# A blocked triangular inverse with two token tiles to a PSUM bank, its transfers on GpSimd's queue, and recurrence decays in tiles of their own

## The chip, the cores and the metric

One core of a Trainium2 chip runs the whole program: four layers of a sequence model on 512 tokens of width 1024. The metric is the device time of one execution in microseconds; the kernel before takes 1904.87 us, the median of three runs (1903.52 to 1909.27).

## What is computed

The first two layers (differential attention and a long convolution) are not touched. Each of the last two has three branches on the same normed input: a gated delta rule (GDN), a causal latent attention (MLA) and a gated linear recurrence (RG-LRU). The parts of the reference that matter:

```python
# gated delta rule, chunks of 64 tokens, 4 heads
a_mat = where(strict, einsum('bnhid,bnhjd->bnhij', kbeta, kc) * decay, 0) + eye(C)
rhs = concatenate([vc * bc, kbeta * exp(gc)[..., None]], axis=-1)
sol = lax.linalg.triangular_solve(a_mat, rhs, lower=True, unit_diagonal=True)
u, w = sol[..., :DV], sol[..., DV:]
...
# rg_lru
r = sigmoid(einsum('bsnc,ncd->bsnd', xb, w_r) + b_r)
i = sigmoid(einsum('bsnc,ncd->bsnd', xb, w_i) + b_i)
log_a = -RG_C * r * softplus(-a_param)
a = exp(log_a)
b = sqrt(-expm1(2.0 * log_a)) * (i * x)
h = associative_scan(a1 * a2, a2 * b1 + b2) over the tokens
```

The kernel solves the triangular system by making the inverse of `a_mat` and multiplying by it. It works on tiles of 128 tokens, so each inverse is 128x128.

## The kernel before, in words

Projections are fp32 split into two parts and multiplied in three passes (`mm3`, L258 to L260); a weight chunk is loaded by SyncE, cast by ScalarE (L266) and its remainder made by VectorE or, for every third chunk, by GpSimd (L267).

In each of the last two layers `layer2` calls `gdn_front`, `lru_open`, `gdn`, `lru`, `mla_v` and `mla` in that order. The framework puts the instructions of each engine in one fixed order before the program runs: by its own estimate of time, an engine takes the ready instruction that was traced earliest. Work that was traced later (projections of `lru`, `mla_v`, `mla`) so fills the places in which earlier work waits. On the chip every engine then follows that order and waits where it must.

The steps around the change, for one layer:

- `solve32` (L1383 to L1401) inverts the 32x32 diagonal blocks on VectorE with 62 small operations (L1398, L1400) and writes them to DRAM (`dm`) by a DMA on ScalarE's queue (L1401).
- `spread` (L1409 to L1427) reads the blocks back by six more DMAs on ScalarE's queue: two into `xd` (L1420), four into `xc` (L1422, named go in the profile). Each moves 64 KB as runs of 32 floats. VectorE then transposes them into `xtc` and the diagonal of `XT` (L1424, L1426).
- `gdn` makes four output gates, then runs `gdn_inv` for the four token tiles (i = 0 to 3) as four generators in turn (`pipeline`, L1474): step 1 of all tiles, then step 2 of all tiles, and so on.
- `gdn_inv` has five steps. Step 1: matmuls L1439 into a bank `lg`, copied by ScalarE (L1441). Step 2: L1445 and L1447 into a bank that the profile calls ft or tr, copied by ScalarE (L1451, L1453), with two small GpSimd operations (L1449, L1450). Step 3: L1457, L1458. Step 4: L1462, L1463. Step 5: L1467, L1471 and their copies. `lg` has two buffers; tr and ft have one each, taken in turn. The matmuls of steps 1, 3 and 4 have 64 columns, those of step 2 have 32, those of step 5 have 128. The first step may not be issued before the last projection of `lru_open` (`self.after(lead)`).
- `lru` takes its four channel chunks in two pairs. Of a chunk: two gate matmuls (L1230, L1233) with a Tanh each (L1232, L1234), Exp for the decay (L1237), Tanh and Sqrt (L1238, L1241), the products (L1235, L1243, L1244), the scan (L1245), a projection for the output gate (L1247, silu at L701 and L702) and the last product (L1250). Tag `l` has three buffers, tag `g2` five, `lw` and bank `av` one each. The decay `dc` has its tile from `g2` and shares it with the second Tanh. The Sqrt of both chunks of a pair are traced together. In `mla` the first user of an `l` tile is L1124.

The lines that the texts below speak of beside these: L1518 (GpSimd, state of the recurrence), L486 (DMAs that GpSimd issues in the first two layers).

Of the kernel before, what the change touches and what calls it, by code (L numbers as in the profile page):

```python
# [12 lines left out]
AF = mybir.ActivationFunctionType  # L13
# [155 lines left out]
class Kern:  # L169
# [1044 lines left out]
    def lru(self, l, h, opened):  # L1214
        nc, A = self.nc, self.A
        bh, sp2, ny, us, conv, _ = opened
        o = self.U()
        for pair in ((0, 1), (2, 3)):
            ts = {}
            for c in pair:  # L1220
                w = self.T("lw", (P, 2, P))
                nc.gpsimd.memset(w, 0.0)
                for q in range(2):
                    r = slice(64 * q, 64 * q + 64)
                    nc.sync.dma_start(w[r, :, r], A[f"lw{l}"][q][:, c])
                if c == 2:
                    conv(3)
                u = us[c]
                pr, pi = self.ps("av"), self.ps("av")
                nc.tensor.matmul(pr, w[:, 0], u, start=True, stop=True)  # L1230
                t, dc = self.T("l"), self.T("g2")
                nc.scalar.activation(t, pr, AF.Tanh, scale=0.5, bias=bh[:, c:c + 1])  # L1232
                nc.tensor.matmul(pi, w[:, 1], u, start=True, stop=True)  # L1233
                nc.scalar.activation(dc, pi, AF.Tanh, scale=0.5, bias=bh[:, 4 + c:5 + c])  # L1234
                nc.vector.scalar_tensor_tensor(u, dc, 1.0, u, op0=ADD, op1=MUL)  # L1235

                nc.scalar.activation(dc, t, AF.Exp, scale=ny[:, c:c + 1], bias=ny[:, c:c + 1])  # L1237
                nc.scalar.activation(t, t, AF.Tanh, scale=sp2[:, c:c + 1], bias=sp2[:, c:c + 1])  # L1238
                ts[c] = t, dc, u
            for t, _, _ in ts.values():  # L1240
                nc.scalar.activation(t, t, AF.Sqrt, scale=0.25)  # L1241
            for c, (t, dc, u) in ts.items():
                nc.vector.scalar_tensor_tensor(t, dc, 1.0, t, op0=ADD, op1=MUL)  # L1243
                nc.gpsimd.tensor_tensor(u, u, t, op=MUL)  # L1244
                nc.vector.tensor_tensor_scan(t, dc, u, 0.0, op0=MUL, op1=ADD)  # L1245
                ps = self.ps("acc")
                self.projT(self.wchunk(A[f"xin{l}"][28 + c], 8, P), h, ps)  # L1247
                gz = self.T("l")
                self.silu2(gz, ps)
                nc.gpsimd.tensor_tensor(o[:, c], t, gz, op=MUL)  # L1250
# [132 lines left out]
    def solve32(self, l, at):  # L1383

        nc = self.nc
        for k in range(4):
            nc.scalar.dma_start(self.blk(self.da[l], k), self.diag(at, k))
        w = self.U()[0:64].rearrange("p (n a) (b i) -> p n (a b) i", n=2, i=32)
        a, m = w[:, 0], w[:, 1]
        flat = lambda t: t.rearrange("p i c -> p (i c)")  # L1390
        nc.scalar.dma_start(flat(a), self.da[l])
        nc.gpsimd.memset(flat(m), 0.0)
        nc.gpsimd.memset(flat(m)[:, 0::33], 1.0)
        tmp = self.T("st", (P, 256))[0:64]
# [14 lines left out]
    def spread(self, l):  # L1409


        nc = self.nc
        xtc, xc = (self.T("go", (P, 16, 32)) for _ in range(2))
        xd = self.T("xd", (P, 16, 64))
        XT = self.T("XT", (P, 4, 4, P))
        nc.gpsimd.memset(XT, 0.0)
        nc.gpsimd.memset(xd, 0.0)
        rs = lambda k: slice(32 * k, 32 * k + 32)
        for k in (0, 2):
            nc.scalar.dma_start(xd[rs(k), :, 16 * k:16 * k + 32], self.blk(self.dm[l], k))  # L1420
        for k in range(4):
            nc.scalar.dma_start(xc[rs(k)], self.blk(self.dm[l], k))  # L1422

        nc.vector.transpose(xtc, xc)  # L1424
        for k in range(4):
            nc.vector.transpose(self.diag(XT, k), xc[rs(k)])  # L1426
        return xd, xc, xtc, XT  # L1427

    def gdn_inv(self, i, at, t1, X, kb, v2, lead):

        nc = self.nc
        mm = nc.tensor.matmul
        ts = slice(i * P, (i + 1) * P)
        xd, xc, xtc, XT = X
        xi = xd[:, 4 * i:4 * i + 4]
        p1 = self.ps("lg", (P, 4, 64))
        with self.after(lead):
            for c in range(4):
                mm(p1[:, c], at[:, i, c], xd[:, 4 * i + c], start=True, stop=True)  # L1439
        for b in (0, 64):  # L1440
            nc.scalar.activation(t1[b + 32:b + 64, i, :, b:b + 32], p1[b + 32:b + 64, :, b // 2:b // 2 + 32], AF.Copy)  # L1441
        yield
        p2 = self.ps("tr", (P, 2, 4, 32))
        for c in range(4):
            mm(p2[:, 0, c], XT[:, i, c], t1[:, i, c, 0:32], start=True, stop=True)  # L1445
        for c in range(4):
            mm(p2[:, 1, c], t1[:, i, c], xtc[:, 4 * i + c], start=True, stop=True)  # L1447

        nc.gpsimd.memset(xi[64:96, :, 32:64], 0.0)  # L1449
        nc.gpsimd.tensor_copy(xi[32:64, :, 32:64], xc[32:64, 4 * i:4 * i + 4])  # L1450
        nc.scalar.activation(xi[32:64, :, 0:32], p2[32:64, 0], AF.Copy, scale=-1.0)  # L1451
        for b in (0, 64):
            nc.scalar.activation(XT[b:b + 32, i, :, b + 32:b + 64], p2[b:b + 32, 1], AF.Copy, scale=-1.0)  # L1453
        yield
        p3 = self.ps("lg", (P, 4, 64))
        for c in range(4):
            mm(p3[:, c], at[:, i, c], xd[:, 4 * i + c], start=True, stop=True)  # L1457
        nc.scalar.activation(t1[64:128, i, :, 0:64], p3[64:128], AF.Copy)  # L1458
        yield
        p4 = self.ps("tr", (P, 4, 64))  # L1460
        for c in range(4):
            mm(p4[:, c], t1[:, i, c], XT[:, i, c, 64:128], start=True, stop=True)  # L1462
        nc.scalar.activation(XT[0:64, i, :, 64:128], p4[0:64], AF.Copy, scale=-1.0)  # L1463
        yield
        pw = self.ps("lg", (P, 4, P))
        for c in range(4):
            mm(pw[:, c], kb[:, i, c], XT[:, i, c], start=True, stop=True)  # L1467
        nc.scalar.activation(kb[:, i], pw, AF.Copy)
        pu = self.ps("tr", (P, 4, P))
        for c in range(4):  # L1470
            mm(pu[:, c], XT[:, i, c], v2[:, c, ts], start=True, stop=True)  # L1471
        nc.scalar.activation(v2[:, :, ts], pu, AF.Copy)

    def pipeline(self, live):  # L1474

        while live:
            live = [g for g in live if next(g, self) is not self]

    def gdn(self, l, h, lead, q2, k2, v2, at, an, kb, egs, ssq, t1, X):
        nc, A = self.nc, self.A  # L1480
        mm = nc.tensor.matmul
        gz = self.U()
        for c in range(4):
            ps = self.ps("acc")
# [14 lines left out]
        for i in range(4):  # L1499
            ts = slice(i * P, (i + 1) * P)  # L1500
            eg = egs[:, i]
            po = self.ps("tr", (P, 4, P))
            for q in range(2):
                hs = slice(2 * q, 2 * q + 2)
                s1 = st[q]
                ps = self.ps("lg", (P, 2, P))
# [25 lines left out]
            r = self.sm(4, "hr")  # L1532
# [129 lines left out]
```

## Time and profile before

| | us |
|---|---|
| median of the runs | 1904.87 (1903.52 to 1909.27) |
| the profiled execution, its own time | 1900.04 |
| its span, first to last instruction | 1898.3 |
| TensorE busy | 1859.4 (98%) |
| VectorE, ScalarE, GpSimd busy | 1246.5, 901.0, 654.3 |
| mean granted TensorE clock | 0.989 |

What lies around the span is 1.7 us. In the profile PE is TensorE's matmul, PEld its weight load, DVE VectorE, ACT ScalarE, POOL GpSimd, SP SyncE; a q behind a name is the engine's sequencer, which issues DMAs and waits. PEclk is the granted clock as a share of full speed: 1.00 is 2.4 GHz, 0.50 is 1.2 GHz.

### The profile page before, as it was taken

The page shows a single profiled execution, that of the slowest core. Times are in us where ns is not written, and L with a number is a line of the kernel's source. Part 1 is how long each engine was busy: PE and PEld are TensorE (multiplying, and loading weights), DVE is VectorE, ACT ScalarE, POOL GpSimd, SP SyncE. Part 2 cuts the span into 40 slices and gives each one's busy share as a digit, 9 for nine tenths or more (in the row PEclk, how much of TensorE's full clock was granted, in tenths as well). Part 3 has the DMA queues.
Part 4 walks back from the last instruction along what each step waited for, and adds up shares of the span by engine and source line. Part 5 has one row for each costly group of instructions (what it writes and reads, how often), then busy time and mean ns, then how long its engine had stood idle before and what let it go on. Part 6 is the DMA issues. An engine that isn't in the chain of part 4 may idle for free.

```text
span 1898.3 us, 26049 instructions
## 1 busy us (share of the span) xinstructions
PE 1859.4 (98%) x9604; PEld 1567.9 (83%) x9604; DVE 1246.5 (66%) x2238; ACT 901.0 (47%) x1761; POOL 654.3 (34%) x552
## 2 busy tenths in 40 slices
PE   8999999999999999999999999999999999999998
PEld 5878888887788788888888788888888887888886
DVE  6888688665788759765567935657235794465723
ACT  4766432324576632223455346656325534765631
POOL 2355343542245534443147323111114642311110
PEclk9999999999999999999999979999999998999999
DMA  5333433224333352333332221213343232022242
GB/s 176 108 111 110 150 113 109 101 89 169 112 99 104 106 169 97 104 100 130 117 103 71 89 61 36 73 59 113 102 136 103 76 89 71 26 76 63 74 133 89
DMA packets 81609, 190.84 MB, mean 101 GB/s; under 512 B 21858, under 2 KB 31843, under 8 KB 81481
## 3 DMA queue, kind: packets, MB, share of 16 engines
q1 hardware_dynamic: 69448, 184.71, 29.8%
q10 hardware_dynamic: 10880, 2.36, 0.7%
q0 software_dynamic: 1152, 2.10, 0.4%
q8 instruction: 76, 1.25, 0.3%
q14 instruction: 53, 0.43, 0.1%
HBM read 171.29 MB, written 17.84 MB: 100 GB/s over the span
## 4 chain that ended last, share of the span: by engine, by line
PE 74%; DVE 14%; issue 4%; ACT 3%; POOL 2%; DMA 2%; ACTq 0%; SPq 0%; DVEq 0%; POOLq 0%
PE acc L260 12%; PE acc L258 12%; PE acc L259 12%; PE fl L260 5%; PE fl L258 5%; PE fl L259 5%; PE av L1181 2%; DVE wl L267 2%; PE av L259 1%; PE av L258 1%; PE av L260 1%; PE lg L260 1%; PE lg L259 1%; PE lg L258 1%; DVE g L1005 1%
## 5 line engine op out<-in xcount | busy, mean ns | idle before, releaser
L266 ACT ACTIVATE wh<-wr 128x1024 fp32r<-128x1024 f32 (+3 forms) x268 | 256.4, 957 | 453.6 <-PE acc L259 165.4
L258 PE MATMUL acc<-u,wh 128*128 128x512 f32 x996 | 394.5, 396 | 0.2
L259 PE MATMUL acc<-u,wh 128*128 128x512 f32 x996 | 393.1, 395 | 0.0
L260 PE MATMUL acc<-u,wl 128*128 128x512 f32 x996 | 393.0, 395 | 0.0
L267 POOL TENSOR_TENSOR wl<-wr,wh 128x1024 fp32r<-128x1024 f32 (+3 forms) x86 | 185.4, 2155 | 498.9 <-ACT wh L266 456.8
L267 DVE TENSOR_TENSOR wl<-wr,wh 128x1024 fp32r<-128x1024 f32 (+3 forms) x182 | 216.0, 1187 | 169.4 <-ACT wh L266 162.1
L258 PEld LDWEIGHTS acc<-u,wh 128*128 128x128 f32 x996 | 187.2, 188 | 41.4 <-issue 2.3
L260 PEld LDWEIGHTS acc<-u,wl 128*128 128x128 f32 x996 | 187.2, 188 | 40.0 <-issue 3.1
L259 PEld LDWEIGHTS acc<-u,wh 128*128 128x128 f32 x996 | 187.3, 188 | 37.1 <-issue 1.4
L258 PE MATMUL fl<-u,wh 128*128 128x512 f32 x316 | 127.7, 404 | 0.0
L260 PE MATMUL fl<-u,wl 128*128 128x512 f32 x316 | 127.1, 402 | 0.0
L259 PE MATMUL fl<-u,wh 128*128 128x512 f32 x316 | 126.9, 402 | 0.0
L260 PE MATMUL acc<-wh,u 128*128 128x512 f32 (+1 forms) x212 | 79.7, 376 | 0.3
L259 PE MATMUL acc<-wl,u 128*128 128x512 f32 (+1 forms) x212 | 79.0, 373 | 0.0
L258 PE MATMUL acc<-wh,u 128*128 128x512 f32 (+1 forms) x212 | 77.7, 374 | 0.6 <-ACT u L266 0.5
L260 PEld LDWEIGHTS fl<-u,wl 128*128 128x128 f32 x316 | 60.4, 191 | 14.0 <-issue 2.0
L258 PEld LDWEIGHTS fl<-u,wh 128*128 128x128 f32 x316 | 60.3, 191 | 14.0 <-issue 2.4
L259 PEld LDWEIGHTS fl<-u,wh 128*128 128x128 f32 x316 | 60.2, 191 | 13.3 <-issue 2.0
L677 ACT ACTIVATE p<-p,mx 128x512 f32<-128x512 f32 x64 | 45.8, 717 | 36.9 <-DVE mx L675 36.6
L790 POOL TENSOR_TENSOR w<-w,ab 128x256 f32<-128x256 f32 x32 | 39.4, 1232 | 68.5 <-DVE w L789 63.3
L321 ACT ACTIVATE sq<-x 128x512 f32<-128x512 f32 x40 | 25.3, 632 | 68.2 <-DVE x L1615 38.1
L1168 ACT ACTIVATE p<-p,amx 128x128 f32<-128x128 f32 (+1 forms) x64 | 35.9, 562 | 30.6 <-DVE amx L1167 29.9
(633 smaller groups left out, 4440.0 us busy)
## 6 DMA issues: line engine op xcount, KB each, us to landing
wr<-in_win SPq DMA_DIRECT2D x88, 512.0 KB, 3.5
wr<-in_xin SPq DMA_DIRECT2D x64, 512.0 KB, 3.5
wr<-in_xout SPq DMA_DIRECT2D x32, 512.0 KB, 3.5
hd<-f SPq DMA_DIRECT2D x32, 256.0 KB, 3.7
hs<-hd SPq DMA_DIRECT2D x32, 256.0 KB, 2.7
wr<-in_wout SPq DMA_DIRECT2D x16, 512.0 KB, 3.4
xd<-x SPq DMA_DIRECT2D x12, 512.0 KB, 3.2
x<-xd SPq DMA_DIRECT2D x12, 512.0 KB, 3.4
```

The lines of the kernel that those rows point to most:

```text
L258: mm(ps, l[0], r[0], start=first, stop=False)
L259: mm(ps, l[0], r[1], start=False, stop=False)
L260: return mm(ps, l[1], r[0], start=False, stop=last)
L266: nc.scalar.activation(hi, src, AF.Copy)
L267: (nc.gpsimd if pool else nc.vector).tensor_tensor(lo, src, hi.bitcast(F32), op=SUB)
L321: self.nc.scalar.activation(self.T("sq"), self.xt(i)[:, h * S:(h + 1) * S], AF.Square, scale=1.0 / math.sqrt(D), accum_out=self.ms2[i][:, ...
L677: nc.scalar.activation(pp[c], pp[c], AF.Exp, bias=mx[:, c:c + 1], accum_out=s0[:, i:i + 1] if c == 0 else s)
L790: nc.gpsimd.tensor_tensor(a[:, 0], a[:, 0], b[:, 1], op=ADD)
L1005: nc.vector.scalar_tensor_tensor(y[:, d:], ps[:, :S - d], w(n), y[:, d:], op0=MUL, op1=ADD)
L1168: nc.scalar.activation(p[:, :n], p[:, :n], AF.Exp, bias=mx, scale=scale, accum_out=s)
L1181: mm(po[:, ts], v[hd // 4][:, k, (hd % 4) * P:(hd % 4 + 1) * P], w[:, k], start=k == 0, stop=k == i)
```

## The change

`gdn_inv` is one function with plain loops: each step runs over the four tiles. For steps 1 to 4 the banks are taken ahead, two for a step, and tiles 0 and 1 share the first, 2 and 3 the second. The seven DMAs of `solve32` and `spread` behind the VectorE part are issued by GpSimd. In `lru` the pairs are gone; a chunk's second Tanh has its tile from `g2` (`ti`) and the decay has one from `l` (`dc`); the Sqrt follows in the chunk. `pipeline` is removed. The numbers of matmuls and copies stay.

```diff
     def lru(self, l, h, opened):
-        for pair in ((0, 1), (2, 3)):
-            ts = {}
-            for c in pair:
+        for c in range(4):
 ...
-                t, dc = self.T("l"), self.T("g2")
+            t, ti, dc = self.T("l"), self.T("g2"), self.T("l")
 ...
-                nc.scalar.activation(dc, pi, AF.Tanh, scale=0.5, bias=bh[:, 4 + c:5 + c])
-                nc.vector.scalar_tensor_tensor(u, dc, 1.0, u, op0=ADD, op1=MUL)
+            nc.scalar.activation(ti, pi, AF.Tanh, scale=0.5, bias=bh[:, 4 + c:5 + c])
+            nc.vector.scalar_tensor_tensor(u, ti, 1.0, u, op0=ADD, op1=MUL)
 ...
-            for t, _, _ in ts.values():
-                nc.scalar.activation(t, t, AF.Sqrt, scale=0.25)
-            for c, (t, dc, u) in ts.items():
-                nc.vector.scalar_tensor_tensor(t, dc, 1.0, t, op0=ADD, op1=MUL)
+            nc.scalar.activation(t, t, AF.Sqrt, scale=0.25)
+            nc.vector.scalar_tensor_tensor(t, dc, 1.0, t, op0=ADD, op1=MUL)
 ...
     def solve32(self, l, at):
 ...
-        nc.scalar.dma_start(self.dm[l], flat(m))
+        nc.gpsimd.dma_start(self.dm[l], flat(m))
 ...
     def spread(self, l):
 ...
         for k in (0, 2):
-            nc.scalar.dma_start(xd[rs(k), :, 16 * k:16 * k + 32], self.blk(self.dm[l], k))
+            nc.gpsimd.dma_start(xd[rs(k), :, 16 * k:16 * k + 32], self.blk(self.dm[l], k))
         for k in range(4):
-            nc.scalar.dma_start(xc[rs(k)], self.blk(self.dm[l], k))
+            nc.gpsimd.dma_start(xc[rs(k)], self.blk(self.dm[l], k))
 ...
-    def gdn_inv(self, i, at, t1, X, kb, v2, lead):
+    def gdn_inv(self, lead, at, t1, X, kb, v2):
 ...
-        p1 = self.ps("lg", (P, 4, 64))
-        with self.after(lead):
-            for c in range(4):
-                mm(p1[:, c], at[:, i, c], xd[:, 4 * i + c], start=True, stop=True)
-        for b in (0, 64):
-            nc.scalar.activation(t1[b + 32:b + 64, i, :, b:b + 32], p1[b + 32:b + 64, :, b // 2:b // 2 + 32], AF.Copy)
-        yield
+        def banks(tag, shape):
+            ps = [self.ps(tag, (P, 2) + shape) for _ in range(2)]
+            return [ps[i // 2][:, i % 2] for i in range(4)]
+
+        p1 = banks("lg", (4, 64))
+        for i in range(4):
+            with self.after(lead):
+                for c in range(4):
+                    mm(p1[i][:, c], at[:, i, c], xd[:, 4 * i + c], start=True, stop=True)
+            for b in (0, 64):
+                cp(t1[b + 32:b + 64, i, :, b:b + 32], p1[i][b + 32:b + 64, :, b // 2:b // 2 + 32], AF.Copy)
+        p2 = banks("tr", (2, 4, 32))
+        for i in range(4):
 ...
+        p3 = banks("lg", (4, 64))
 ...
+        p4 = banks("tr", (4, 64))
 ...
-        self.pipeline([self.gdn_inv(i, at, t1, X, kb, v2, lead) for i in range(4)])
+        self.gdn_inv(lead, at, t1, X, kb, v2)
```

Steps 2 to 4 are cut above; they take their banks in the same way and are otherwise those of before.

## Rows read from the trace of the kernel before

**Rows 1.** The page: the granted TensorE clock in 40 slices, in tenths.

```profile
PEclk9999999999999999999999979999999998999999
```

**Rows 2.** Windows: stretch, length, busy us (count) of PE, PEld, DVE, ACT, POOL; PEclk; DMA share; GB/s.

```profile
1100.00:1150.00 50.00, 47.68 (x266) 41.62 (x265) 15.24 (x19) 29.00 (x54) 12.85 (x16) 0.80 0.15 39
1550.00:1600.00 50.00, 47.87 (x225) 39.83 (x223) 35.61 (x70) 17.83 (x29) 11.39 (x13) 0.94 0.35 99
1600.00:1650.00 50.00, 50.00 (x296) 42.86 (x297) 17.10 (x26) 34.73 (x62) 14.26 (x12) 0.89 0.06 17
1109.50:1122.00 12.50, 11.53 (x44) 10.21 (x45) 3.08 (x3) 6.95 (x17) 3.64 (x5) 0.50 0.16 43
1122.90:1126.50 3.60, 3.60 (x33) 3.60 (x33) 0.69 (x1) 1.40 (x4) 1.26 (x1) 0.97 0.00 0
1126.50:1132.50 6.00, 6.00 (x20) 4.68 (x20) 0.55 (x1) 2.25 (x6) 0.32 (x1) 0.50 0.00 0
```

**Rows 3.** Timeline of PE, 1100 to 1137 us: start, duration, line, tiles, count, idle before.

```profile
1100.94 1.90 PE L1439 MATMUL lg<-xd,at 128*128 128x64 f32 x16
...
1107.66 0.41 PE L1445 MATMUL ft<-X,XT 128*128 128x32 f32 x2 [0.91 <-ACT X L1441]
...
1110.47 1.97 PE L1439 MATMUL lg<-xd,at 128*128 128x64 f32 x8 [1.42 <-ACT X L1441]
...
1124.67 1.06 PE L1445 MATMUL tr<-X,XT 128*128 128x32 f32 x8
...
1134.54 1.89 PE L1457 MATMUL lg<-xd,at 128*128 128x64 f32 x16
```

**Rows 4.** Timeline of ACT, 1098 to 1116 us.

```profile
1098.89 2.14 ACTq L1422 DMA_DIRECT2D go<-dm  x4
1101.13 1.06 ACT L266 ACTIVATE wh<-wr 128x1024 fp32r<-128x1024 f32 x1 [5.02 <-issue]
...
1105.64 0.82 ACT L1237 ACTIVATE g<-l,ny 128x512 f32<-128x512 f32 x1 [2.88 <-DVE lu L1235]
...
1107.92 1.28 ACT L1241 ACT_TABLE_LOAD   x1
...
1115.41 0.27 ACT L1451 ACTIVATE xd<-ft 32x128 f32<-32x128 f32 x1 [2.38 <-PE ft L1447]
```

**Rows 5.** Waits of PE in the second of the two layers, 1572 to 1640 us.

```profile
PE lg L1439 <- ACT X L1441: 1.4, 1, 1.4
PE ft L1445 <- ACT X L1441: 0.7, 1, 0.7
```

**Rows 6.** Timeline of DVE, 1101 to 1105 us.

```profile
1101.31 2.13 DVE L1426 STREAM_TRANSPOSE XT<-go 32x512 f32<-32x512 f32 x3 [4.69 <-DMA go<-dm]
...
1104.91 0.69 DVE L1235 SCALAR_TENSOR_TENSOR lu<-g,lu 128x512 f32<-128x512 f32 x1
```

**Rows 7.** DMAs by issuing engine, whole run: issue ns (min/median/max); then time to landing.

```profile
L1422 ACTq DMA_DIRECT2D go<-dm x8: 499/510/763, 1098.9 to 1583.3; - x8
...
L486 POOL DMA_DIRECT2D x<-in_fltb x4: 537/584/782, 14.7 to 468.2; - x4
...
dm<-u ACTq DMA_DIRECT2D x2, 256.0 KB, 2.9
...
x<-in_fltb POOLq DMA_DIRECT2D x4, 256.0 KB, 3.5
```

**Rows 8.** Timeline of POOL, 1095 to 1105 us, and the last product of `lru`.

```profile
1094.95 1.55 POOL L1518 TENSOR_TENSOR st<-st,eg 128x256 f32<-128x256 f32 x1 [11.96 <-DVE u L1400]
1102.26 2.39 POOL L267 TENSOR_TENSOR wl<-wr,wh 128x1024 fp32r<-128x1024 f32 x1 [5.77 <-DMA go<-dm]
...
1171.27 1.29 POOL L1250 TENSOR_TENSOR u<-l,l 128x512 f32<-128x512 f32 x1 [2.01 <-DVE l L702]
```

**Rows 9.** The first ACT instruction of `mla` on an `l` tile; table loads, both layers.

```profile
1194.78 0.62 ACT L1124 ACTIVATE l<-g 64x512 fp32r<-64x512 f32 x1
...
L1241 ACT ACT_TABLE_LOAD x8 | 10.3, 1283 | 0.1
```

More of the change, by code (lines that the diff above doesn't have):

```diff
@@ L1217, in lru @@
         o = self.U()
-        for pair in ((0, 1), (2, 3)):
-            ts = {}
-            for c in pair:
[L1221 to L1230, printed above, removed]
-                t, dc = self.T("l"), self.T("g2")
-                nc.scalar.activation(t, pr, AF.Tanh, scale=0.5, bias=bh[:, c:c + 1])
-                nc.tensor.matmul(pi, w[:, 1], u, start=True, stop=True)
-                nc.scalar.activation(dc, pi, AF.Tanh, scale=0.5, bias=bh[:, 4 + c:5 + c])
-                nc.vector.scalar_tensor_tensor(u, dc, 1.0, u, op0=ADD, op1=MUL)
-                nc.scalar.activation(dc, t, AF.Exp, scale=ny[:, c:c + 1], bias=ny[:, c:c + 1])
-                nc.scalar.activation(t, t, AF.Tanh, scale=sp2[:, c:c + 1], bias=sp2[:, c:c + 1])
-                ts[c] = t, dc, u
-            for t, _, _ in ts.values():
-                nc.scalar.activation(t, t, AF.Sqrt, scale=0.25)
-            for c, (t, dc, u) in ts.items():
-                nc.vector.scalar_tensor_tensor(t, dc, 1.0, t, op0=ADD, op1=MUL)
[L1244 to L1250, printed above, removed]
@@ new lines, in lru @@
+        for c in range(4):
+            w = self.T("lw", (P, 2, P))
+            nc.gpsimd.memset(w, 0.0)
+            for q in range(2):
+                r = slice(64 * q, 64 * q + 64)
+                nc.sync.dma_start(w[r, :, r], A[f"lw{l}"][q][:, c])
+            if c == 2:
+                conv(3)
+            u = us[c]
+            pr, pi = self.ps("av"), self.ps("av")
+            nc.tensor.matmul(pr, w[:, 0], u, start=True, stop=True)
+            t, ti, dc = self.T("l"), self.T("g2"), self.T("l")
+            nc.scalar.activation(t, pr, AF.Tanh, scale=0.5, bias=bh[:, c:c + 1])
+            nc.tensor.matmul(pi, w[:, 1], u, start=True, stop=True)
+            nc.scalar.activation(ti, pi, AF.Tanh, scale=0.5, bias=bh[:, 4 + c:5 + c])
+            nc.vector.scalar_tensor_tensor(u, ti, 1.0, u, op0=ADD, op1=MUL)
+            nc.scalar.activation(dc, t, AF.Exp, scale=ny[:, c:c + 1], bias=ny[:, c:c + 1])
+            nc.scalar.activation(t, t, AF.Tanh, scale=sp2[:, c:c + 1], bias=sp2[:, c:c + 1])
+            nc.scalar.activation(t, t, AF.Sqrt, scale=0.25)
+            nc.vector.scalar_tensor_tensor(t, dc, 1.0, t, op0=ADD, op1=MUL)
+            nc.gpsimd.tensor_tensor(u, u, t, op=MUL)
+            nc.vector.tensor_tensor_scan(t, dc, u, 0.0, op0=MUL, op1=ADD)
+            ps = self.ps("acc")
+            self.projT(self.wchunk(A[f"xin{l}"][28 + c], 8, P), h, ps)
+            gz = self.T("l")
+            self.silu2(gz, ps)
+            nc.gpsimd.tensor_tensor(o[:, c], t, gz, op=MUL)
@@ L1427, in spread @@
         return xd, xc, xtc, XT
-    def gdn_inv(self, i, at, t1, X, kb, v2, lead):
+    def gdn_inv(self, lead, at, t1, X, kb, v2):
         nc = self.nc
         mm = nc.tensor.matmul
-        ts = slice(i * P, (i + 1) * P)
+        cp = nc.scalar.activation
         xd, xc, xtc, XT = X
-        xi = xd[:, 4 * i:4 * i + 4]
-        p1 = self.ps("lg", (P, 4, 64))
-        with self.after(lead):
-            for c in range(4):
-                mm(p1[:, c], at[:, i, c], xd[:, 4 * i + c], start=True, stop=True)
-        for b in (0, 64):
-            nc.scalar.activation(t1[b + 32:b + 64, i, :, b:b + 32], p1[b + 32:b + 64, :, b // 2:b // 2 + 32], AF.Copy)
-        yield
-        p2 = self.ps("tr", (P, 2, 4, 32))
-        for c in range(4):
[L1445 to L1472, printed above, removed]
@@ L1474, in pipeline @@
-    def pipeline(self, live):
-        while live:
-            live = [g for g in live if next(g, self) is not self]
+        def banks(tag, shape):
[8 more added lines that the diff above has]
+                cp(t1[b + 32:b + 64, i, :, b:b + 32], p1[i][b + 32:b + 64, :, b // 2:b // 2 + 32], AF.Copy)
@@ new lines, in gdn_inv @@
+        p2 = banks("tr", (2, 4, 32))
+        for i in range(4):
+            for c in range(4):
+                mm(p2[i][:, 0, c], XT[:, i, c], t1[:, i, c, 0:32], start=True, stop=True)
+            for c in range(4):
+                mm(p2[i][:, 1, c], t1[:, i, c], xtc[:, 4 * i + c], start=True, stop=True)
+            xi = xd[:, 4 * i:4 * i + 4]
+            nc.gpsimd.memset(xi[64:96, :, 32:64], 0.0)
+            nc.gpsimd.tensor_copy(xi[32:64, :, 32:64], xc[32:64, 4 * i:4 * i + 4])
+            cp(xi[32:64, :, 0:32], p2[i][32:64, 0], AF.Copy, scale=-1.0)
+            for b in (0, 64):
+                cp(XT[b:b + 32, i, :, b + 32:b + 64], p2[i][b:b + 32, 1], AF.Copy, scale=-1.0)
@@ new lines, in gdn_inv @@
+        p3 = banks("lg", (4, 64))
+        for i in range(4):
+            for c in range(4):
+                mm(p3[i][:, c], at[:, i, c], xd[:, 4 * i + c], start=True, stop=True)
+            cp(t1[64:128, i, :, 0:64], p3[i][64:128], AF.Copy)
+        p4 = banks("tr", (4, 64))
+        for i in range(4):
+            for c in range(4):
+                mm(p4[i][:, c], t1[:, i, c], XT[:, i, c, 64:128], start=True, stop=True)
+            cp(XT[0:64, i, :, 64:128], p4[i][0:64], AF.Copy, scale=-1.0)
@@ L1479, in gdn @@
+        for i in range(4):
+            ts = slice(i * P, (i + 1) * P)
+            pw = self.ps("lg", (P, 4, P))
+            for c in range(4):
+                mm(pw[:, c], kb[:, i, c], XT[:, i, c], start=True, stop=True)
+            cp(kb[:, i], pw, AF.Copy)
+            pu = self.ps("tr", (P, 4, P))
+            for c in range(4):
+                mm(pu[:, c], XT[:, i, c], v2[:, c, ts], start=True, stop=True)
+            cp(v2[:, :, ts], pu, AF.Copy)
     def gdn(self, l, h, lead, q2, k2, v2, at, an, kb, egs, ssq, t1, X):
```

## The prediction

> **What bounds the kernel now.** I read the table of times first: TensorE is busy for 1859.4 of 1898.3 us, so the end moves only by what TensorE waits, what its clock loses, or what it has to do more. Then the clock on the page [rows 1]: it is full almost everywhere and falls in two places, once in each of the last two layers. The windows show these places at 1100 to 1150 us and 1550 to 1650 us [rows 2]. Granted clock times length gives what they lose: 0.20 of 50 us = 10.0 us in the third layer, (0.06 + 0.11) of 50 us = 8.5 us in the fourth. The clock has two levels there, 1.00 (2.4 GHz) and 0.50 (1.2 GHz): 1109.5 to 1122 us lies at 0.50 throughout.
>
> What stands there is the blocked inverse [rows 3]: matmuls of 64 and 32 columns in place of the projections' 512. TensorE also sits idle twice, 0.91 and 1.42 us, until ScalarE has copied a result of step 1 (L1441); in the fourth layer it is 0.7 and 1.4 us [rows 5]. No other wait of TensorE is listed there, so 2.3 + 2.1 = 4.4 us of idle time and 18.5 us of clock are all that this stretch could give back.
>
> Why ScalarE is late is in its timeline [rows 4]. It issues the block DMAs and is idle for 5.02 us before L266. Its Exp (L1237) waits 2.88 us more for a product on VectorE (L1235), which stands behind five transposes that wait 4.69 us for the same DMAs [rows 6]. Then a table load (1.28 us) for Sqrt stands between the copies of tiles 0 and 1. The first 16 matmuls of step 1 were over at 1102.8 us; the copies of tile 1 come after that table load and its Sqrt.
>
> The chip's work is the same in both layers, so each step below is worked out for one and doubled or added.
>
> **The change part by part.** *The transfers leave ScalarE.* Seven issues, each about 0.5 us [rows 7], and the waits for the landings between them leave its queue: the 5.02 us. Its Tanh (L1234) could then run as soon as its matmul has ended, some 4 us earlier, L1235 goes into VectorE's 4.69 us of idle time ahead of the transposes, and Exp, Tanh, table load and Sqrt are done before step 1 has ended. The copies then follow their matmuls. That takes out both idle places: -2.3 us and -2.1 us. What is late next is the transfer itself.
>
> *They come to GpSimd's queue.* No row shows such a DMA from GpSimd. Below: as from ScalarE, 0, since GpSimd is idle for 5.77 us there [rows 8], and seven issues at the 0.58 us of L486 [rows 7] are 4.1 us. Above: the first issue stands behind the product at L1518 (1.55 us), the landing takes 3.5 us in place of 2.9 us (both 256 KB), and the issue could go with the number of runs: L486 moves 128 runs of 2 KB, a block read 512 runs of 128 bytes, so four times 0.58 = 2.3 us, 1.8 us more than ScalarE's 0.51 us, six times. That is 1.6 + 0.6 + 10.8 = 13 us a layer. ScalarE's rows speak for the low end, so I take 0.58 us: the blocks land 1.6 + 0.6 + 0.4 = 2.6 us later. Behind the waiting issues stand a weight split (L267, 2.39 us), the memset of the next `lw`, and L1449 and L1450. The cover is TensorE's wide work: it lasted until 1106.75 us, the transposes until 1104.9 us, 1.9 us earlier, and an order made for the later blocks would put more projections ahead. I cost it at 0; uncovered it is 0.7 us a layer.
>
> The Trainium skill ("DMA: Bandwidth & Descriptors", section "Issuing engine by pattern") speaks against this part: plain loads belong on a hardware-generated queue, which it calls generally faster, with a first byte after some 0.6 us against 1 us. By that the chain of two dependent transfers would be an estimated 0.8 us longer, and the sum 1.6 us worse; L486's landing beside ScalarE's points the same way.
>
> *Two tiles to a bank.* It looks as if step 1 of all tiles could now run at once. The rows say no: L1451 reads only what L1445 wrote, yet it waits for L1447, the later half of the same bank [rows 4]. An access waits for the other engine's work on its bank. So tile 1 will wait for tile 0's copy, and tile 3 for tile 2's; before, tile 2 waited for tile 0 and tile 3 for tile 1. Two waits a step, as before; the order becomes 0, 2, 1, 3. Cost 0. Bounds: -1.4 us a layer, the wait before the third tile [rows 3], and as much the other way; the first part has taken that wait already.
>
> *Step by step.* The generators went round the tiles in turn, so this was the order already: 0.
>
> *The decays.* Sqrt had a table load for each of its eight chunks [rows 9], so the pairing saved none: 0. `dc` now takes the third `l` buffer, so chunk c+1's decay waits for the end of chunk c. That slows the recurrence branch, but its last product was at 1171.3 us [rows 8] and `mla` first needs an `l` buffer at 1194.8 us [rows 9]: 22 us of cover. If that is gone, every further microsecond delays the first head of `mla`, though not its projections. 0; bounds 0 and a few microseconds.
>
> *The clock.* It lost 10.0 and 8.5 us for the same order of work; the idle places are part of what preceded the fall. Bounds: all of it back (-18.5 us), or the narrow work closes up (below). I take the better layer's value for both: -1.5 us.
>
> Sum: -2.3 - 2.1 - 1.5 = -5.9 us. Against the profiled execution's 1900.0 us that is 1894.1 us; the median of the runs stands 4.8 us above that execution, so the forecast is **1899.0 us**, with 1894 to 1903 as its own range: the clock term from 0 to -5 with half to all of the idle time.
>
> **The rivals.** *The clock stays up.* If the fall comes of the idle places, all of the clock's loss goes with them: 1904.9 - 4.4 - 18.5 = 1882 us. Against it: 1122.9 to 1126.5 us is narrow work without a gap (3.60 of 3.60 us busy), and the clock falls right behind it [rows 2]. Chance 0.17. The Trainium skill ("TensorE: Matmul & The Clock Gate", section "HAM oscillation") blames gaps in TensorE's work; by that rule this rival would be the forecast, and the trace agrees only for the first fall.
>
> *The bank pairing really closes the steps up.* With a ScalarE that is never late, fewer projections stand between the narrow matmuls. At full clock 16 of 64 columns take 1.9 us, 8 of 32 columns 1.06 us [rows 3]; a layer has 32 in each of steps 1, 3 and 4 and 64 in step 2, so 3.8 x 3 + 8.5 = 20 us. With 3.6 us of it at full clock and the rest at half, the loss is 16.3 us a layer, or 12.5 us if step 1 stands apart. That is 6.5 to 14 us worse over both layers than now, less 4.4 us of idle time: 1907 to 1915 us. Chance 0.18, two thirds of it for the lower end.
>
> *GpSimd's issues are slow (the slower one).* If an issue takes twice L486's, the blocks are 2.6 + 6 x 0.58 = 6.1 us later; past 1.9 us TensorE stands before L1445 with nothing wide left in its order: 4.2 us a layer, 8.4 us: 1913 us. It decides from an issue of about 0.6 us on if the order doesn't make room; at the upper bound it is 1927 us. For it: the two transfers are on the chain. Against it: 0.58 us in the rows. Chance 0.20.
>
> That the change doesn't do what it says is in the second and third parts: neither the steps nor the banks are new to the order.
>
> **How the numbers follow.** Forecast 0.45. A measurement of this kernel can tell about 0.3%, 5.7 us. The forecast's own range lies half below 1899.2 us: 0.23; with the rival of the clock faster is 0.40. Within 0.3%: the other half, 0.22, and the lower end of the bank rival, 0.12: 0.34. Slower: GpSimd 0.20 and the upper end, 0.06: 0.26. The range of 1882 to 1914 us leaves out half of the outer two and a little more, some 0.2.
>
> **What would show it.** Right: no idle place of TensorE before L1439 and L1445, ScalarE without an idle place put down to issue, L1441 right behind L1439, the GpSimd DMAs at about 0.6 us each, and clocks about 0.83 in the two windows. Wrong: TensorE idle before L1445 until VectorE's L1426, DMA issues over 1 us, an idle place before L1148 or L1159, or a clock that stays at 1.00 or loses 12 us and more a layer.

## The result and the profile after

The changed kernel takes 1892.41 us (median of six runs, 1890.34 to 1894.3) against 1903.8 us (six runs, 1899.94 to 1909.27): a ratio of 0.994, 95% interval 0.9923 to 0.9958. That is 11.4 us faster; the forecast was 5.9. The profiled execution took 1893.08 us, its span is 1891.3 us at a mean granted clock of 0.992 (before: 1900.04, 1898.3, 0.989).

The page's clock row of the changed kernel, and its windows in the three stretches of [rows 2]:

```profile
PEclk9999999999999999999999989999999998999999
```

```profile
1100.00:1150.00 50.00, 49.94 (x307) 43.45 (x306) 18.45 (x21) 31.39 (x58) 17.31 (x23) 0.90 0.18 51
...
1550.00:1600.00 50.00, 49.94 (x250) 41.77 (x248) 34.58 (x62) 24.06 (x41) 15.62 (x21) 0.92 0.29 89
1600.00:1650.00 50.00, 48.79 (x292) 41.78 (x292) 20.36 (x31) 30.92 (x57) 14.95 (x14) 0.94 0.09 24
```

TensorE has lost its idle time in the first two (49.94 of 50 us busy, before 47.68 and 47.87). The clock loses 5.0 us in the third layer and 4.0 + 3.0 us in the fourth, 12.0 in place of 18.5 us. It still falls in each layer, though no gap of TensorE stands among the narrow matmuls (those of 32 or 64 columns) any more. TensorE's timeline in the third layer, the answer to [rows 3]:

```profile
1103.56 1.97 PE L1440 MATMUL lg<-xd,at 128*128 128x64 f32 x16
...
1109.10 1.90 PE L1440 MATMUL lg<-xd,at 128*128 128x64 f32 x16
1110.83 1.03 PE L1446 MATMUL ft<-X,XT 128*128 128x32 f32 x8
1111.70 1.06 PE L1448 MATMUL ft<-go,X 128*128 128x32 f32 x8
1112.59 1.06 PE L1446 MATMUL tr<-X,XT 128*128 128x32 f32 x8
1113.48 1.08 PE L1448 MATMUL tr<-go,X 128*128 128x32 f32 x8
1114.38 2.06 PE L1228 MATMUL av<-lu,lw 128*128 128x512 f32 x2
```

No wait stands in it. The clock halves behind 48 narrow matmuls without a gap: the two gate matmuls behind them take 2.06 us (1.02 us at full clock). Before, it was at half from 1109.5 us on [rows 2], inside the second idle place, and most of step 2 ran at 1.89 us for eight. ScalarE and GpSimd over the same time, the answers to [rows 4] and [rows 8]:

```profile
1094.17 0.82 ACT L1235 ACTIVATE l<-l,ny 128x512 f32<-128x512 f32 x1
...
1095.86 1.28 ACT L1237 ACT_TABLE_LOAD   x1
...
1104.67 0.55 ACT L1442 ACTIVATE X<-lg 32x128 f32<-32x128 f32 x2 [2.73 <-PE lg L1440]
1105.57 0.55 ACT L1442 ACTIVATE X<-lg 32x128 f32<-32x128 f32 x2 [0.34 <-PE lg L1440]
```

```profile
1096.90 0.66 POOL L1396 DMA_DIRECT2D dm<-u  x1 [12.18 <-DVE u L1395]
...
1100.21 1.39 POOL L1415 DMA_DIRECT2D xd<-dm  x2 [1.98 <-DMA dm<-u]
1101.59 2.58 POOL L1417 DMA_DIRECT2D go<-dm  x4
1104.15 0.33 POOL L1220 MEMSET lw<- 128x256 f32 x1
1104.42 2.40 POOL L267 TENSOR_TENSOR wl<-wr,wh 128x1024 fp32r<-128x1024 f32 x1
```

Exp, the table load and Sqrt of the first chunk are over by 1097.8 us, before step 1 begins, and the copies (L1442) come right behind their matmuls. An issue of GpSimd takes 0.66 us for `dm`, 0.70 and 0.65 us for a block. One wait of TensorE is new. It stands in the fourth layer, ahead of a projection behind `lru` (at 1644.30 us), whose `acc` bank was still being read by the product L702 of `lru`'s last output gate:

```profile
PE acc L258 <- DVE l L702: 1.2, 1, 1.2
```

### The profile page after: what moved, and what is told of

The parts are those of the page before. It is cut to its first block, busy times and chain, and to the rows that moved or that the text cites. A ratio compares the mean times of both kernels' runs of the same rounds, so it can differ in the third digit from the quotient of the medians.

```text
span 1891.3 us, 26054 instructions
## 1 busy us (share of the span) xinstructions
PE 1854.0 (98%) x9604; PEld 1560.9 (83%) x9604; DVE 1254.6 (66%) x2238; ACT 900.1 (48%) x1761; POOL 659.9 (35%) x566
## 4 chain that ended last, share of the span: by engine, by line
PE 75%; DVE 13%; issue 4%; ACT 3%; POOL 3%; DMA 2%; ACTq 0%; SPq 0%; DVEq 0%; POOLq 0%
PE acc L258 13%; PE acc L260 13%; PE acc L259 13%; PE fl L259 5%; PE fl L258 5%; PE fl L260 5%; PE av L1181 2%; DVE wl L267 2%; DVE g L1005 1%; PE av L259 1%; PE av L258 1%; PE av L260 1%; PE av L588 1%; PE lg L259 1%; PE lg L260 1%
## 5 line engine op out<-in xcount | busy, mean ns | idle before, releaser
L267 POOL TENSOR_TENSOR wl<-wr,wh 128x1024 fp32r<-128x1024 f32 (+3 forms) x86 | 186.2, 2165 | 490.1 <-ACT wh L266 451.0
L267 DVE TENSOR_TENSOR wl<-wr,wh 128x1024 fp32r<-128x1024 f32 (+3 forms) x182 | 217.5, 1195 | 170.0 <-ACT wh L266 159.6
L258 PEld LDWEIGHTS fl<-u,wh 128*128 128x128 f32 x316 | 60.1, 190 | 13.2 <-issue 1.5
```

The costliest lines, as they stand in the source:

```text
L258: mm(ps, l[0], r[0], start=first, stop=False)
L267: (nc.gpsimd if pool else nc.vector).tensor_tensor(lo, src, hi.bitcast(F32), op=SUB)
```

## The experiments

Each run lists its span and mean granted clock, so a span can be split: span x (1 - clock) is what the clock cost, span x clock is the rest, idle time in it. The clock has three decimals, so one run's split is good to 1 us; idle time at half clock counts half in each term. The last two columns are means over the runs, in us, with twice their standard error. Each ratio is to the runs of the kernel before that were made beside it and need not be the quotient of two medians; the first row has one such set of them (in the other sets the clock loss is 22.9 to 23.9 us).

| kernel | runs | median us | ratio to before, 95% | clock loss | rest |
|---|---|---|---|---|---|
| before | 23 | 1903.55 | 1 | 23.6 ± 1.4 | 1877.9 ± 0.5 |
| changed kernel | 6 | 1892.41 | 0.9940 (0.9923 to 0.9958) | 15.4 ± 2.3 | 1875.1 ± 1.2 |
| d_transfers | 6 | 1891.90 | 0.9938 (0.9920 to 0.9956) | 15.4 ± 3.0 | 1874.9 ± 0.9 |
| r_decays | 12 | 1901.68 | 0.9990 (0.9977 to 1.0003) | 18.1 ± 2.1 | 1881.5 ± 0.6 |
| b_banks | 12 | 1903.34 | 1.0004 (0.9990 to 1.0018) | 24.3 ± 1.8 | 1878.5 ± 0.6 |
| dr_no_banks | 6 | 1889.39 | 0.9922 (0.9903 to 0.9941) | 13.2 ± 3.1 | 1874.0 ± 1.1 |
| s_sync | 12 | 1901.58 | 0.9994 (0.9983 to 1.0004) | 22.5 ± 1.7 | 1877.6 ± 0.6 |
| bo_product_first | 11 | 1905.34 | 1.0016 (1.0006 to 1.0026) | 23.9 ± 1.8 | 1880.0 ± 0.8 |
| so_sync_product_first | 8 | 1896.45 | 0.9970 (0.9958 to 0.9982) | 19.7 ± 2.7 | 1874.7 ± 0.7 |
| late_copies | 11 | 1909.06 | 1.0022 (1.0011 to 1.0033) | 25.6 ± 2.2 | 1880.0 ± 1.1 |
| w64_step2 | 4 | 1880.96 | 0.9880 (0.9864 to 0.9896) | 3.8 ± 2.2 | 1875.4 ± 0.1 |
| w128_steps | 4 | 1879.85 | 0.9871 (0.9854 to 0.9888) | 3.8 ± 2.2 | 1874.0 ± 1.9 |
| bw_before_wide | 6 | 1890.78 | 0.9936 (0.9921 to 0.9950) | 7.6 ± 4.4 | 1881.7 ± 1.0 |
| dw_transfers_wide | 5 | 1881.48 | 0.9882 (0.9864 to 0.9900) | 3.8 ± 1.7 | 1876.4 ± 1.0 |

By this split the change is worth -8.2 us of clock and -2.8 us of the rest.

### The three parts, one by one

**d_transfers**: the kernel before with this part of the diff alone.

```diff
-        nc.scalar.dma_start(self.dm[l], flat(m))
+        nc.gpsimd.dma_start(self.dm[l], flat(m))
...
-            nc.scalar.dma_start(xd[rs(k), :, 16 * k:16 * k + 32], self.blk(self.dm[l], k))
+            nc.gpsimd.dma_start(xd[rs(k), :, 16 * k:16 * k + 32], self.blk(self.dm[l], k))
...
-            nc.scalar.dma_start(xc[rs(k)], self.blk(self.dm[l], k))
+            nc.gpsimd.dma_start(xc[rs(k)], self.blk(self.dm[l], k))
```

> The kernel before with the seven block transfers alone moved to GpSimd's queue. Theory 1 (the issues and landings stood ahead of ScalarE's copies): about -8 to -11 us against the kernel before, the whole of the change; both idle places of TensorE in the inverse (0.91 and 1.42 us in the third layer, 0.7 and 1.4 us in the fourth) are gone, and some of the 18.5 us of clock loss with them. Theory 2 (the decays' own tile freed ScalarE's Exp): ScalarE's Exp still waits for VectorE's product of the same chunk, the copies stay late, and this run gives less than -3 us. The clock loss of the two stretches (18.5 us before, 12.0 us after) tells where the rest lies.

Measured: 0.9938, both terms of the split as in the changed kernel. This part is the whole result.

**r_decays**: the kernel before with the new `lru`.

```diff
-                t, dc = self.T("l"), self.T("g2")
+            t, ti, dc = self.T("l"), self.T("g2"), self.T("l")
...
-            for t, _, _ in ts.values():
-                nc.scalar.activation(t, t, AF.Sqrt, scale=0.25)
+            nc.scalar.activation(t, t, AF.Sqrt, scale=0.25)
```

> The kernel before with the recurrence's new order alone (dc in a tile of l, Sqrt per chunk); transfers still on ScalarE. Theory 1: the 5.02 us of ScalarE's idle time ahead of the Tanh and its issues stay, so the idle places stay within half, and the time is within 3 us of the kernel before. Theory 2: Exp no longer waits 2.88 us for VectorE's product, one Sqrt with its table load moves, and at least half of the 11.4 us is here: -6 us or more.

Measured: 0.999, no difference that can be told. But it is a sum of two: the rest is 3.6 us longer and the clock loses 5.5 us less. Exp no longer waits for the product, as theory 2 had it, yet the freed chain only meets the next wait. The waits of TensorE, whole run, in this kernel:

```profile
PE av L1228 <- issue: 8.1, 2, 4.2
```

TensorE stands 4.2 us once a layer, ahead of the second chunk's gates, behind the first half of step 1: 8.1 us new in place of the 4.4 us that are gone, which is the longer rest. The profile names no releaser. By the times it is the first chunk's second Tanh, the last reader of the one bank `av`, which now stands behind the table loads for Sqrt and back; it ends 0.1 us before the gates start. ScalarE, then TensorE:

```profile
1109.45 0.69 ACT L1232 ACTIVATE g<-av,bh 128x512 f32<-128x512 f32 x1
```

```profile
1110.24 2.04 PE L1228 MATMUL av<-lu,lw 128*128 128x512 f32 x2 [4.24 <-issue]
```

These gates run at half clock, 2.04 us in place of 1.02: the clock falls over this gap too, though wide matmuls alone follow it.

**b_banks**: the kernel before with the new `gdn_inv`.

```diff
-        self.pipeline([self.gdn_inv(i, at, t1, X, kb, v2, lead) for i in range(4)])
+        self.gdn_inv(lead, at, t1, X, kb, v2)
```

> The kernel before with the inverse's new banks and step order alone. Both theories: nothing, within 2 us of the kernel before, the two idle places of TensorE before the later tiles of step 1 still there. The rival, that the banks close the steps up: narrow matmuls stand closer, the stretch at half clock is longer, +3 to +8 us. The other way, that the bank order spares the wait before the third tile: -3 us.

Measured: 1.0004, and TensorE's two waits are those of [rows 5] in both layers:

```profile
PE lg L1445 <- ACT X L1447: 2.8, 2, 1.4
...
PE ft L1451 <- ACT X L1447: 1.7, 2, 0.9
```

Neither banks nor step order change anything here. The bank rival spoke of a ScalarE that is never late, which this kernel doesn't have; the next one tries that.

**dr_no_banks**: the changed kernel with the old `gdn_inv`.

> The changed kernel without its new banks and step order (transfers on GpSimd and the recurrence's new order stay). If the banks are neutral: within 2 us of the changed kernel, -9 to -13 us against the kernel before, no idle time of TensorE in the inverse. If the bank order is what took the idle places away: they are back, and the time is -2 to -7 us.

Measured: 0.9922, its interval overlapping the changed kernel's: 3.3 ± 3.7 us under it by the means, so with ScalarE on time the banks cost nothing that can be told, and the bank rival (1907 us and more) is off. It showed something else. In its fourth layer TensorE's order is that of the changed kernel from the first half of step 1 to the end of step 2's first half, at the same distances, and yet the clock stays up in one execution and falls in the other. First this kernel, then the changed one:

```profile
1589.45 1.06 PE L1440 MATMUL tr<-X,XT 128*128 128x32 f32 x8
1590.35 1.06 PE L1442 MATMUL tr<-go,X 128*128 128x32 f32 x8
```

```profile
1588.68 1.76 PE L1446 MATMUL tr<-X,XT 128*128 128x32 f32 x8
1590.25 1.89 PE L1448 MATMUL tr<-go,X 128*128 128x32 f32 x8
```

The two kernels differ in their banks, but the runs of one kernel, whose order is fixed, spread in the same way: here from 1883.92 us at a clock of 0.996 to 1893.27 us at 0.992. So whether the clock falls is not settled by the order alone, and one profile is no measure of the clock term.

### Why it takes GpSimd's queue

**s_sync**: d_transfers with `nc.sync` in place of `nc.gpsimd` in the same three lines.

> The kernel before with the seven block transfers alone on SyncE's queue. Theory 1a (it is enough that ScalarE's queue holds no transfer): as d_transfers, -8 to -13 us against the kernel before, TensorE's idle time in the inverse under 0.5 us a layer. Theory 1b (it takes the later landing of GpSimd's transfers, which puts step 1 behind more of the projections' matmuls and ScalarE's table load and Sqrt ahead of both first copies): here the copy of tile 1 stands behind the table load and Sqrt as it did before, step 1 starts at about 1101 us as before, idle places of 1 us and more stay in each layer, and the time is within 4 us of the kernel before.

Measured: 0.9994, nothing. ScalarE holds no transfer any more, but its Exp waits longer than before (2.88 us, [rows 4]), and TensorE still waits for the copies. The waits of TensorE, then ScalarE and VectorE of this kernel:

```profile
PE lg L1439 <- ACT X L1441: 2.6, 2, 1.3
```

```profile
1099.54 0.69 ACT L1234 ACTIVATE g<-av,bh 128x512 f32<-128x512 f32 x1
1107.61 0.82 ACT L1237 ACTIVATE g<-l,ny 128x512 f32<-128x512 f32 x1 [7.38 <-DVE lu L1235]
...
1109.88 1.28 ACT L1241 ACT_TABLE_LOAD   x1
```

```profile
1103.28 2.13 DVE L1426 STREAM_TRANSPOSE XT<-go 32x512 f32<-32x512 f32 x3 [4.83 <-DMA go<-dm]
...
1106.88 0.69 DVE L1235 SCALAR_TENSOR_TENSOR lu<-g,lu 128x512 f32<-128x512 f32 x1
```

The order of VectorE is fixed before the program runs, and here, as before [rows 6], it has the product L1235 behind the transposes that wait for the blocks. With the transfers on GpSimd's queue it comes out with the product first (that the plan counts on the blocks later there is my reading, not shown). VectorE in d_transfers:

```profile
1101.84 0.69 DVE L1235 SCALAR_TENSOR_TENSOR lu<-g,lu 128x512 f32<-128x512 f32 x1 [1.81 <-ACT g L1234]
1105.67 2.16 DVE L1426 STREAM_TRANSPOSE XT<-go 32x512 f32<-32x512 f32 x3 [3.14 <-DMA go<-dm]
```

So theory 1a (it is enough to rid ScalarE of the transfers) falls. Theory 1b (the product's place on VectorE) was tested by itself.

**bo_product_first**: the kernel before, with only an edge that orders VectorE.

```diff
-        nc.vector.transpose(xtc, xc)
+        self.trs = [nc.vector.transpose(xtc, xc)]
...
-                nc.vector.scalar_tensor_tensor(u, dc, 1.0, u, op0=ADD, op1=MUL)
+                pr = nc.vector.scalar_tensor_tensor(u, dc, 1.0, u, op0=ADD, op1=MUL)
+                if c == 0:
+                    for t1 in self.trs:
+                        self.tc.add_manual_dep(t1.ins, pr.ins.name, mybir.DependencyInfo(mybir.DependencyClass.NoSync, mybir.DependencyReason.DATA), reason="order")
```

> The kernel before with one thing added: an ordering edge that puts VectorE's product of the recurrence's first chunk (L1235) ahead of the five transposes that wait for the block transfers. No transfer is moved, ScalarE still issues all seven; the order that follows has the table load and Sqrt ahead of both first copies, and 16 of the projections' matmuls between the halves of step 1. Theory 1b (VectorE's order is the cause, the queue of the transfers only brought it about): Exp no longer waits 2.88 us, TensorE's idle time in the inverse falls under 1 us a layer, clock loss to about 15 us, and the time is -7 to -12 us against the kernel before, as d_transfers. Theory 1a (ScalarE has to be rid of the issues and landings): its 5.02 us of idle time stays and the copies stay late, within 4 us of the kernel before.

Measured: 1.0016, slightly slower. Theory 1b falls too, as it stood. The product is first, but Exp still waits 2.48 us for it, and TensorE up to 3.0 us for a copy. The waits of TensorE, ScalarE, VectorE and GpSimd:

```profile
PE lg L1442 <- ACT X L1444: 5.8, 2, 3.0
```

```profile
1103.43 0.67 ACT L1234 ACTIVATE g<-av,bh 128x512 f32<-128x512 f32 x1
1106.58 0.81 ACT L1240 ACTIVATE g<-l,ny 128x512 f32<-128x512 f32 x1 [2.48 <-DVE lu L1235]
```

```profile
1104.13 2.41 DVE L1235 SCALAR_TENSOR_TENSOR lu<-g,lu 128x512 f32<-128x512 f32 x1 [6.11 <-ACT g L1234]
```

```profile
1103.60 2.40 POOL L267 TENSOR_TENSOR wl<-wr,wh 128x1024 fp32r<-128x1024 f32 x1 [5.71 <-DMA go<-dm]
```

The product lasts 2.41 us in place of 0.69; GpSimd's weight split has begun before it (more on this in the last section). And the Tanh that it needs still stands behind the issues.

**so_sync_product_first**: both edits, SyncE's queue and the edge.

> s_sync with the same ordering edge: transfers on SyncE's queue, VectorE's product ahead of the transposes. In s_sync Exp waited 7.38 us for that product. Theory 1b: the wait goes, and with it the idle places; -8 to -13 us against the kernel before, as d_transfers or a little better, since step 1 starts no later than in s_sync. If the time stays where s_sync has it (within 4 us of the kernel before), neither the queue nor this order is the cause and it is the later place of step 1 on GpSimd's queue.

Measured: 0.997. The rest is now that of d_transfers (1874.7 against 1874.9 us): the waits on ScalarE's copies are gone. It takes both, a ScalarE without transfers and a product that doesn't wait for them. The product still meets the split (2.52 us, below), and two waits of up to 1.1 us for `lw` come in, whose transfers share SyncE's queue with the blocks. The clock loss is 19.7 us, between s_sync's and d_transfers', so the two edits bring back some 6 of the 11 us; why the clock gives less here is open. VectorE, then the waits of TensorE in this kernel:

```profile
1101.00 2.52 DVE L1235 SCALAR_TENSOR_TENSOR lu<-g,lu 128x512 f32<-128x512 f32 x1 [1.81 <-ACT g L1234]
```

```profile
PE av L1230 <- DMA lw<-in_lw: 1.6, 2, 1.1
```

GpSimd's queue brings a third thing: its own issues hold back the split, which starts at 1106.11 us in d_transfers, long after the product. What that is worth by itself no run shows. GpSimd in d_transfers:

```profile
1103.28 2.56 POOL L1422 DMA_DIRECT2D go<-dm  x4
...
1106.11 2.39 POOL L267 TENSOR_TENSOR wl<-wr,wh 128x1024 fp32r<-128x1024 f32 x1
```

### What makes the clock fall

**late_copies**: d_transfers with a ScalarE that is late again.

```diff
+        if i == 0:
+            for f in (AF.Sqrt, AF.Tanh) * 3:
+                nc.scalar.activation(t1[32:64, i, :, 0:32], p1[32:64, :, 0:32], f, scale=0.0)
```

> d_transfers with ScalarE made late again: six small activations with five table loads of 1.28 us stand ahead of tile 0's copies in step 1, some 8 us (5 x 1.28 + 6 x 0.27), with 21 projections' matmuls in place of 16 to cover them. TensorE's idle time should come back, 3 to 5 us a layer. Theory A (idle places among the narrow matmuls are what makes the clock fall): the clock loss goes back from 15 us to 24 us or more as well, in all +14 to +19 us against d_transfers. Theory B (the clock falls for the run of narrow matmuls itself, and an idle place adds nothing): the idle time alone, +6 to +10 us against d_transfers, with the clock loss at 13 to 18 us.

Measured: 1909.06 us, 17.2 us above d_transfers by the medians, 15.3 by the means: the clock loss is 10.2 us up, at 25.6, and the rest 5.1 us. The idle time is 2.9 us a layer, between narrow matmuls; the waits of TensorE, whole run:

```profile
PE ft L1448 <- ACT X L1444: 5.7, 2, 2.9
```

That is theory A's number: a gap among the narrow matmuls costs more than itself. The edit also puts a gate pair and eight matmuls of step 1 ahead of the gap, so gap and order were not tried apart. r_decays stands 4.2 us a layer, with one wide matmul between step 1's first half and the gap and only wide ones right behind it, and loses no more than 18.1 us, so the place seems to count too.

**w64_step2** and **w128_steps**: dr_no_banks with wider matmuls, which compute every column twice and use one half. In step 2:

```diff
-        p2 = self.ps("tr", (P, 2, 4, 32))
+        p2 = self.ps("tr", (P, 2, 4, 2, 32))
+        twice = lambda t: t.unsqueeze(1).to_broadcast([P, 2, 32])
...
-            mm(p2[:, 0, c], XT[:, i, c], t1[:, i, c, 0:32], start=True, stop=True)
+            mm(p2[:, 0, c], XT[:, i, c], twice(t1[:, i, c, 0:32]), start=True, stop=True)
```

w128_steps does the same with 64 columns in steps 1, 3 and 4.

> dr_no_banks with the matmuls of step 2 made 64 columns wide in place of 32, by reading the moving operand twice; results are taken from one half. Rows at full clock give 8 matmuls of 32 columns and 8 of 64 columns the same 1.06 us, so the pace itself should not move. Theory C (it is the few columns for which the clock falls): the clock loss sinks from 13 us to under 7 us, and the time is -4 to -10 us against dr_no_banks, near 1882 us. Theory D (the clock falls for these matmuls whatever their width): within 2 us of dr_no_banks. A third way: at half clock the wider ones take longer, +2 to +5 us.

> As w64_step2, and the matmuls of steps 1, 3 and 4 made 128 columns wide in place of 64 in the same way; step 5 has 128 columns already. Theory C: no fall of the clock is left in the inverse of either layer, the loss of the two stretches goes from 5 to 12 us to under 2 us, and the time is about 1880 us. Theory D: within 2 us of dr_no_banks. The third way, wider at half clock: +4 to +10 us.

Measured: 0.988 and 0.9871; theory C. The clock loss goes from 13.2 to 3.8 us in both, and no fall is left in the inverse. Windows and TensorE of w128_steps:

```profile
1100.00:1150.00 50.00, 49.78 (x340) 44.03 (x339) 21.17 (x26) 32.49 (x61) 21.22 (x26) 1.00 0.18 51
...
1550.00:1600.00 50.00, 49.72 (x282) 42.07 (x281) 32.56 (x56) 28.31 (x50) 17.94 (x24) 1.00 0.29 88
1600.00:1650.00 50.00, 50.00 (x320) 43.82 (x319) 24.08 (x43) 30.85 (x65) 15.30 (x15) 1.00 0.12 34
```

```profile
1112.66 1.06 PE L1442 MATMUL tr<-X,XT 128*128 128x64 f32 x8
...
1127.73 1.06 PE L1459 MATMUL ft<-XT,X 128*128 128x128 f32 x8
```

Eight matmuls take 1.06 us with 32, 64 or 128 columns, so the added columns cost nothing at full clock. The order shifts a little with it (5 and 14 projections' matmuls in place of 4 and 11 between the later narrow groups). Up to the end of step 2's first half, where the clock fell before, it is the same. w128_steps beats both kernels: 23 us under the runs of the kernel before beside it (1902.82 us), with an interval (0.9854 to 0.9888) wholly below the changed kernel's.

**bw_before_wide**: the same widening in the kernel before, nothing else.

> The kernel before with the widening of w128_steps alone: step 2 at 64 columns, steps 1, 3 and 4 at 128, by reading the moving operand twice. Transfers, banks, recurrence and the two idle places of TensorE stay as before. Theory C (few columns are what the clock falls for; the idle places only add to it): clock loss from 23.6 us to under 8 us with the idle places still there at 2.3 and 2.1 us, time -13 to -19 us against the kernel before. Theory A alone (the idle places are what makes it fall): the loss stays at 20 us or more and the time within 4 us of the kernel before, or above it.

Measured: 0.9936, the worth of the whole change with none of its parts. Both idle places are there, in the waits of TensorE:

```profile
PE lg L1440 <- ACT X L1442: 2.7, 2, 1.4
...
PE ft L1447 <- ACT X L1442: 1.6, 2, 0.9
```

The clock loss falls to 7.6 us (22.9 us in the kernel before beside it), but not in every run: three runs stand at 1886.3 to 1888.2 us (clock 0.997 to 0.999), the others higher, up to 1897.92 us. In the profiled execution it fell in both layers. So neither theory is the whole: narrow matmuls and gaps among them each add to the fall, and with one of the two gone it comes less often. The rest is some 4 us longer than before. In the trace 1.7 us of it are two new waits ahead of L1542 (1.0 and 0.7 us); the other half is not explained.

**dw_transfers_wide**: d_transfers with the widening.

> d_transfers with the widening of w128_steps: of the change's three parts only the transfers on GpSimd, no new recurrence, no new banks. If the recurrence's new order adds nothing once the transfers are moved: within 3 us of w128_steps (1879.9 us), clock loss under 6 us, idle time of the inverse gone. If the recurrence's tiles are needed to keep ScalarE ahead of the copies: the Exp's wait for VectorE's product (0.76 us in d_transfers) grows back, idle places come back and the time is 4 us or more above w128_steps.

Measured: 0.9882, 1.6 us above w128_steps with overlapping intervals. Once the transfers are moved the recurrence's new order adds nothing that can be told. Four kernels now make a square. The clock loss is 23.6 us with gaps and narrow matmuls, 15.4 us without the gaps (d_transfers), 7.6 us without the narrow matmuls (bw_before_wide) and 3.8 us without either. Moving the transfers changes TensorE's order a little as well, so its side of the square is not the gaps alone.

## Why the prediction was right, and where it was not

The direction and the wide range, 1882 to 1914 us, held; the forecast's own range, 1894 to 1903 us, did not, the measured 1892.41 us lying 1.6 us under it. Step by step:

- **The transfers leave ScalarE (-4.4 us of idle time).** The idle places went, as put; the rest of the span gave 2.8 ± 1.3 us, 1.2 us of the difference being the new wait in the fourth layer. The reason given was wrong in one place: that L1235 "goes into VectorE's 4.69 us of idle time ahead of the transposes" once Tanh can run early. In s_sync Tanh ran early and L1235 stayed behind the transposes. An idle engine in a fixed order doesn't take what is ready; the move to GpSimd's queue changed that order. In the changed kernel it doesn't even matter, since `dc` has a tile of its own and Exp runs before the product.
- **GpSimd's queue (0, at 0.58 us an issue).** 0.65 to 0.70 us measured, above the 0.6 us from which the slower rival was to decide "if the order doesn't make room". It did make room, and in d_transfers the queue held a weight split away from the product, which the prediction listed only as a cost. The Trainium skill ("DMA: Bandwidth & Descriptors", "Issuing engine by pattern") calls SyncE's kind of queue generally faster. On the chain the traces agree: from the issue of `dm` to the first transpose it takes 6.55 us on SyncE's queue and 7.09 us on GpSimd's. The time was not decided by that: it is 0.9994 on SyncE's queue, 0.997 there with the edge, and 0.9938 on GpSimd's.
- **Two tiles to a bank, and step by step (0 and 0).** Right: 1.0004 alone. Step 1 still comes in two halves of 16 matmuls, at 1103.56 and 1109.10 us, as the reading of the bank has it; that the order of the tiles became 0, 2, 1, 3 is not shown.
- **The decays (0).** Right as a sum, 0.999 alone. It hid +3.6 us of rest and -5.5 us of clock. That `dc` frees Exp from VectorE, and that in r_decays the Sqrt of the first chunk comes ahead of its second Tanh, by the times of which the bank `av` comes free late, was not seen.
- **The clock (-1.5 us).** The term that was mis-sized: -8.2 us over the runs. "I take the better layer's value for both" read one execution's 8.5 us as what the order costs, where executions of one kernel differ by as much. The windows were to show about 0.83; they show 0.90, 0.92 and 0.94.

The sum was -5.9 us; with the measured terms it is -2.8 - 8.2 = -11.0, against 11.4 between the medians. So most of the gain came from the term that the forecast held to be small, and that the total lay within the wide range is partly luck. The rival of the clock had the right mechanism in part. Without idle places the clock still falls, and the 18.5 us don't all come back; but three quarters of the gain are its kind. The Trainium skill's rule ("TensorE: Matmul & The Clock Gate", "HAM oscillation"), which blames gaps, agrees in kind with late_copies (+10.2 us of clock loss for 5.7 us of gaps). It doesn't cover bw_before_wide, where some 15 us of the loss go with the gaps in place.

## What to carry to other kernels

Where each engine's order is made ahead from estimates, moving a transfer to another queue is also an edit of every order that waits for it: look at what stands behind the waiting instruction, and try the queue and the order apart. Split spans by the granted clock over several runs before judging a change of some tenths of a per cent. Where matmuls keep their pace at more columns, try the wider form before rearranging work around a clock that falls; here the bank pairing of this change stands in its way, since a bank that holds two tiles of 4 x 64 floats then holds one of 4 x 128.

## What was not expected of the hardware

- Matmuls of 32, 64 and 128 fp32 columns have one pace at full clock, 1.06 us for eight, and the narrow ones are those behind which the clock falls without a gap: 23.6 us of loss before, 3.8 us with the wide form and the transfers moved.
- The same matmuls in the same order ran at full clock in an execution of dr_no_banks and at half in one of the changed kernel (1.06 against 1.89 us for eight), and the runs of dr_no_banks alone spread from a clock of 0.996 to 0.991.
- A VectorE product of 0.69 us took 2.41, 2.52 and, in the changed kernel, 2.69 us where GpSimd's split L267 had begun before it, and ended some 0.55 us after it. The Trainium skill ("SBUF — State Buffer", "Who interferes with whom") says that such a pair excludes one another and that the one issued first keeps the other out; these rows agree.

The row of the changed kernel for the last point:

```profile
1104.70 2.69 DVE L1233 SCALAR_TENSOR_TENSOR lu<-g,lu 128x512 f32<-128x512 f32 x1
```
